# Hybrid state-space and attention block: three portions of a group's small work, at the ends of whole weight pieces

## The chip, the cores and the metric

The kernel runs on one core of one Trainium2 chip. The time is that of one execution in device microseconds (us), given as the median of several runs; the profile is of one execution. PE is the engine that multiplies matrices (PEld its weight loads), DVE is VectorE, ACT is ScalarE, POOL is GpSimd, and SP issues the DMAs.

## The reference

One transformer-like block over 512 tokens of width 1024, in float32. The part that the change touches is the state space branch; around it stand a three-group dilated attention, two gates and a feed-forward part with a short convolution.

```python
h = rms_norm(x, norm1_g)
z, xbc, dt_raw, q, k, v, g_ssd, g_attn = jnp.split(h @ w_in, IN_SPLITS, axis=-1)
# state space branch, 8 groups of 4 heads of 64, state 128, chunks of 128 tokens
xbc = silu(causal_dwconv(xbc, conv_w, conv_b))          # xs, Bm, Cm
dt = softplus(dt_raw + dt_bias)
CB = einsum('bclgn,bcsgn->bcgls', Cc, Bc)               # per group and chunk
y_diag = einsum('bcgkls,bcsgkp->bclgkp', CB[:, :, :, None] * Ldec, X)
states = einsum('bclgn,bcgkl,bclgkp->bcgkpn', Bc, decay_states, X)
prev = scan over the chunks: carry * chunk_decay + states
y_off = einsum('bclgn,bcgkpn,bcgkl->bclgkp', Cc, prev, exp(a_cs))
y = (y_diag + y_off + d_skip * xs) * silu(z)
y_ssd = rms_norm over each group's 256 channels
# the rest
merged = sigmoid(g_ssd) * (y_ssd @ w_ssd_proj) + sigmoid(g_attn) * (y_attn @ w_attn_proj)
x = x + merged @ w_out
x = x + (silu(u_gate) * u_val) @ w_down                 # u: convolved rms_norm(x) @ w_up
```

## The kernel before

**Large matmuls.** All weights come in pieces (512 KB here). SP loads a piece (`raw`, three buffers), ACT rounds it to `whi` (L104), and DVE takes the rest, `wlo = raw - whi` (L105); both have three buffers and are made up to two pieces ahead (`prefetch`). The activations are split into `hh` and `hl` in the same way. A piece of 128 output channels is then 24 matmuls of 128x128 by 512 tokens into one of four PSUM banks "mm": whi with hh, whi with hl, wlo with hh, eight each (`mm_chan`, L144).

**The state space stage.** The loop over `g` (8 groups) takes six pieces a group: B, C, two of x, two of z (`ps_ssd`). At the end of a piece, ACT and DVE bring the result out of PSUM; for B, C and x this is the convolution (`conv4`: one step on ACT, three on DVE, the latter shown as L52). Silu follows per pair (`silus`). Behind the eight groups stand 16 gate pieces (`ps_gate`); the first six of them are still run beside the small work, and then `finish` runs what is left of it.

**The small work of a group** is the generator `ssd_side`, with ps_cb (C with B, L714), ps_bt and ps_xt (transposes of B and x, L720 and L733), ps_st (states, L745), ps_y and ps_o (the two parts of the result for each half j, L764 and L769: y0, o0, y1, o1) and ps_n (the sum of squares for the norm, L785 and L786). The DVE steps between them are the subtraction that begins the decay matrix (`bc`, also called `mt` and `m4`, L705), `cbm` (L715), the product of the two (L723), `xdt` and `xdc` (L736, L739), the recurrence `prev` (L750 to L754) and four steps per half of y (L52, L772 to L774). ACT does Relu and Exp on the decay (L707, L708). The PSUM banks of the small work are two "tr" and two "aux".

**What sets the order.** PE runs its instructions in exactly the order in which the program is written (`manual_schedule` names PE). For the other engines and SP's queue, a scheduler at build time lays down an order from its own estimate of when operands are there, with the program's order as priority. All engines then work through their own list in order.

**Ticks.** Small work is put between large matmuls by `tick`, which advances every active generator whose wait is over; `yield k` means "go on k ticks later". A piece has two ticks, one after its 12th matmul and one at its end. Counted from a group's first piece, odd ticks fall into the middle of a piece, even ones at its end; 1 to 12 lie in the group's own pieces and 13 to 24 in those of the next group. With `GN = (7, 2, 2)`, `YL` and `NL`, a group from the third on has: 1 subtraction, 2 Relu and Exp, 9 cb and bt, 10 product, 12 and 13 xt, 14 st, 16 y0 and o0, 19 y1 and o1, 21 the decay loads for the group two further on (`load_decay`, one of 1 MB and two of 256 KB, two buffers each) and the sum of squares on POOL, 22 its split `sr`, 25 n, 27 and 28 the DMA back and the power on POOL. The first two groups start late and have numbers of their own (`G0`, `G1`), and the third starts four ticks late (`G2W`). The combination of the three attention groups (`combine`) starts `COMB` ticks after the last attention chain; it consists of 12 products with loaded factors (L645), 8 sums (L647) and 4 splits (L651 and L653), with the transposes ps_fT ahead of them. It runs beside the first groups of the state space stage.

Of the kernel before, what the change touches and what calls it, by code (L numbers as in the profile page):

```python
# [16 lines left out]
P = 128  # L17
S = 512
NT = S // P
# [4 lines left out]

LAG, PVLAG = 2, 2
LAUNCH = (12, 5, 13)
COMB = 11
G0, G1, GN = (2, 1, 1, 1), (5, 2, 4, 2), (7, 2, 2)
G2W, YL = 4, 3
NL = (1, 3, 2, 1)  # L30

Z0, XS0, B0, C0, DT0 = 0, 2048, 4096, 5120, 6144
Q0, K0, V0, GS0, GA0 = 6176, 7712, 9248, 10784, 11808
# [5 lines left out]
def kernel(  # L39
# [6 lines left out]
    nc = tc.nc  # L46
# [649 lines left out]
    def ssd_side(g, bct, xst, zs, at):  # L696
        sp = late["b"]

        def T(tag, shape, bufs=1):
            return sp.tile(shape, F32, tag=tag, name=f"{tag}_{g}", bufs=bufs)  # L700

        hs = slice(4 * g, 4 * g + 4)
        mt, eb = decay[g]
        m4 = mt.rearrange("p h (c l) -> p h c l", c=NT)
        nc.vector.tensor_sub(m4, acs[:, :, hs].rearrange("p c h -> p h c").unsqueeze(3).broadcast_to((P, 4, NT, P)), m4)  # L705
        yield 1
        nc.scalar.activation(mt, mt, AF.Relu)  # L707
        nc.scalar.activation(mt, mt, AF.Exp, scale=-1.0)  # L708
        yield at["cb"]
        cbm = T("cbm", [P, NT, P])  # L710
        ps = bank("aux", f"ps_cb{g}")
        for c in range(NT):
            cs = slice(c * P, (c + 1) * P)
            nc.tensor.matmul(ps[:, cs], bct[:, 0, cs], bct[:, 1, cs], start=True, stop=True)  # L714
        nc.vector.tensor_mul(cbm, ps.rearrange("p (c l) -> p c l", c=NT),  # L715
                             triu.unsqueeze(1).broadcast_to((P, NT, P)))
        btok = T("btok", [P, 3, P])
        ps = bank("tr", f"ps_bt{g}")
        for c in range(3):
            nc.tensor.transpose(ps[:, c * P:(c + 1) * P], bct[:, 0, c * P:(c + 1) * P], ident)  # L720
        nc.scalar.copy(btok.rearrange("p c n -> p (c n)"), ps[:, :3 * P])
        yield 1
        nc.vector.tensor_mul(m4, m4, cbm.unsqueeze(1).broadcast_to((P, 4, NT, P)))  # L723
        yield at["x"]
        xdt = T("xdt", [P, NT, 4, 64])
        xdc = T("xdc", [P, 3, 4, 64])
        for hf in range(2):
            ps = bank("tr", f"ps_xt{g}_{hf}")
            for c in range(2):
                for j in range(2):  # L730
                    o = c * 256 + j * P
                    t0 = (2 * hf + c) * P
                    nc.tensor.transpose(ps[:, o:o + P], xst[:, j, t0:t0 + P], ident)  # L733
            p4 = ps.rearrange("p (c h d) -> p c h d", c=2, h=4)
            cc = slice(2 * hf, 2 * hf + 2)
            nc.vector.tensor_mul(xdt[:, cc], p4, dtt[:, cc, hs].unsqueeze(3).broadcast_to((P, 2, 4, 64)))  # L736
            n = 2 - hf
            cc = slice(2 * hf, 2 * hf + n)
            nc.vector.tensor_mul(xdc[:, cc], p4[:, :n], dtd[:, cc, hs].unsqueeze(3).broadcast_to((P, n, 4, 64)))  # L739
            yield 1  # L740
        prev = T("prev", [P, 3, 4, 64])
        pst = [bank("aux", f"ps_st{g}_{i}") for i in range(2)]
        sts = [pst[c // 2][:, c % 2 * 256:c % 2 * 256 + 256] for c in range(3)]
        for c in range(3):
            nc.tensor.matmul(sts[c], btok[:, c, :], xdc[:, c].rearrange("p h d -> p (h d)"),  # L745
                             start=True, stop=True)
        for c in range(3):
            p3 = sts[c].rearrange("p (h d) -> p h d", h=4)
            if c == 0:
                nc.vector.tensor_copy(prev[:, 0], p3)  # L750
            else:
                nc.vector.tensor_mul(prev[:, c], prev[:, c - 1],
                                     cdec[:, c, hs].unsqueeze(2).broadcast_to((P, 4, 64)))
                nc.vector.tensor_add(prev[:, c], prev[:, c], p3)  # L754
        yield at["y"]
        sq = T("sq", [P, 2, S])
        for j in range(2):
            b = 2 * g + j
            y = ysb[:, b, :]
            psy = bank("aux", f"ps_y{g}_{j}")  # L760
            for c in range(NT):
                cs = slice(c * P, (c + 1) * P)
                for i in range(2):
                    nc.tensor.matmul(psy[i * 64:(i + 1) * 64, cs], xdt[:, c, 2 * j + i, :],  # L764
                                     mt[:, 2 * j + i, cs], start=True, stop=True)
            pso = bank("aux", f"ps_o{g}_{j}")
            for c in range(1, NT):
                cs = slice(c * P, (c + 1) * P)
                nc.tensor.matmul(pso[:, cs], prev[:, c - 1, 2 * j:2 * j + 2, :].rearrange("p h d -> p (h d)"),  # L769
                                 bct[:, 1, cs], start=True, stop=True)  # L770
            stt(y, xst[:, j, :], dsk[:, b:b + 1], psy, ALU.mult, ALU.add)
            nc.vector.tensor_mul(sq[:, j, P:], pso[:, P:], eb[:, j, P:])  # L772
            nc.vector.tensor_add(y[:, P:], y[:, P:], sq[:, j, P:])
            nc.vector.tensor_mul(y, y, zs[:, j, :])  # L774
            nc.scalar.activation(sq[:, j, :], y, AF.Square)
            yield YL - j
        load_decay(g + 2)
        nc.gpsimd.tensor_add(sq[:, 0, :], sq[:, 0, :], sq[:, 1, :])
        yield NL[0]
        sr = sp.tile([P, 2, S], F32R, tag="sr", name=f"sr_{g}", bufs=1)  # L780
        nc.scalar.copy(sr[:, 0, :], sq[:, 0, :])
        nc.gpsimd.tensor_sub(sr[:, 1, :], sq[:, 0, :], sr[:, 0, :].bitcast(F32))
        yield NL[1]
        ps = bank("aux", f"ps_n{g}")
        nc.tensor.matmul(ps[0:1, :], ones_r, sr[:, 0, :], start=True, stop=False)  # L785
        nc.tensor.matmul(ps[0:1, :], ones_r, sr[:, 1, :], start=False, stop=True)  # L786
        vv = T("vv", [1, S])
        nc.scalar.activation(vv, ps[0:1, :], AF.Identity, bias=epsb[0:1], scale=1.0 / 256)
        nc.sync.dma_start(scr_v[g], vv)
        yield NL[2]  # L790
        rv = T("rv", [P, NT], 2)
        nc.sync.dma_start(rv, scr_v[g].rearrange("(p c) -> p c", c=NT))
        yield NL[3]
        nc.gpsimd.tensor_tensor(rv, rv, nhalf.broadcast_to((P, NT)), op=ALU.pow)
        nc.sync.dma_start(scr_r[g].rearrange("(p c) -> p c", c=NT), rv)
# [3 lines left out]
            nc.scalar.activation(o, o, AF.Silu)  # L799
        yield 1  # L800

    normal = dict(zip(("cb", "x", "y"), GN))
    tiles = {}

    def branch_tiles(g):
# [3 lines left out]
    for g in range(8):  # L809
        if g > 1:  # L810
            branch_tiles(g)
        if g > 1:
            start(ssd_side(g, *tiles[g], normal), G2W if g == 2 else 0)
        banks = []
        for i in range(6):
            w = next_piece()
            banks.append(bank("mm", f"ps_ssd{g}_{i}"))
            mm_chan(banks[i], w, hh, hl)
            if (g, i) == (0, 1):
                ab_cm.__exit__(None, None, None)  # L820
                late["a"] = sa_cm.__enter__()
                branch_tiles(0)
            if (g, i) != (0, 0):
                bct, xst, zs = tiles[g]
                for k in ((0, 1) if (g, i) == (0, 1) else (i,)):
                    if k < 2:
                        conv4(banks[k], 16 + 8 * k + g, bct[:, k, :])
                    elif k < 4:
                        conv4(banks[k], 2 * g + k - 2, xst[:, k - 2, :])
                    else:  # L830
                        nc.scalar.copy(zs[:, k - 4, :], banks[k])
            if i % 2 and g > 0:
                start(silus(tiles[g][i // 2]), 1)
            tick()
            if (g, i) == (0, 4):
                assert not any(s[0].__name__ in ("chain", "launch") for s in sides)
                aa_cm.__exit__(None, None, None)
                ap = ap_cm.__enter__()
                for k in "hl":
                    merged[k] = ap.tile([P, 4, S], F32R, tag="a" + k, name="a" + k)  # L840
                sb_cm = pool("ssd_b", side="right")
                late["b"] = sb_cm.__enter__()
                load_decay(0)
                load_decay(1)
                start(ssd_side(0, *tiles[0], dict(zip(("cb", "x", "y"), G0))), G0[3])
            if (g, i) == (0, 5):
                start(ssd_side(1, *branch_tiles(1), dict(zip(("cb", "x", "y"), G1))), G1[3])
                start(silus(*tiles[0]), 1)


# [572 lines left out]
```

## Time and profile before

| | |
|---|---|
| median of 3 runs | 1215.61 us (1214.03 to 1215.69) |
| profiled execution | 1215.73 us, span 1214.0 us |
| busy PE / PEld | 1201.3 / 1001.8 us |
| busy DVE / ACT / POOL | 756.7 / 574.4 / 140.9 us |
| mean granted clock of PE | 0.996 |
| HBM traffic | 133.22 MB read, 4.70 MB written, 114 GB/s |

A view of groups or of the timeline names line, engine, operation, what is written and read (out<-in, by the program's names), the shapes and the count. "idle before" is time in which the engine had nothing under way, and what follows the arrow is what ended it. A matmul in full float32 appears as two records, one for each pass; the large ones are of a rounded type and appear as one. The end of a matmul is modelled and reaches past the start of the next, so that a row of n matmuls is measured better from start to start. The chain of waits follows the work that ended last back through the execution, and its pieces are laid end to end.

### The profile page before, as it was taken

Reading aid. Unit: us, or ns where it says so; the run is one execution under the profiler, and the core shown is the slowest. Engines: PE = TensorE matmul, PEld = TensorE weight load, DVE = VectorE, ACT = ScalarE, POOL = GpSimd, SP = SyncE. Lnnn points to the kernel's source line nnn. Section 1 sums busy time; section 2 is a strip of 40 time slices with the busy share of each in tenths; the row PEclk is TensorE's granted clock in tenths of the full one; section 3 lists DMA queues with packets and bytes.
Section 4 is the critical chain, followed back from the end, with each engine's and each line's share of the span. In section 5 each row is a group of like instructions: output and inputs, shape, how many; then the busy total and the mean of one; then the engine's idle time right before and its main releaser. Section 6 shows DMA issues by size and latency. Waiting matters only on the chain.

```text
span 1214.0 us, 15957 instructions
## 1 busy us (share of the span) xinstructions
PE 1201.3 (99%) x6316; PEld 1001.8 (83%) x6316; DVE 756.7 (62%) x999; ACT 574.4 (47%) x890; POOL 140.9 (12%) x95
## 2 busy tenths in 40 slices
PE   9999989999999999999999999999999999999998
PEld 7877767998888888888888888888888999988887
DVE  5214354356789977777744354654779888885542
ACT  4434456367746655465433333433554444444431
POOL 1011111100000201101011000000224242300000
PEclk9999989999999999999999999999999999999999
DMA  5444534422646544424235423344324242425330
GB/s 185 122 106 97 129 97 108 106 72 71 178 126 179 149 121 122 139 71 139 74 81 133 130 88 103 98 143 159 124 76 129 82 114 85 122 87 174 104 121 35
DMA packets 177163, 138.95 MB, mean 114 GB/s; under 512 B 12416, under 2 KB 150256, under 8 KB 176065
## 3 DMA queue, kind: packets, MB, share of 16 engines
q1 hardware_dynamic: 177089, 137.94, 40.2%
q8 instruction: 49, 0.80, 0.3%
q14 instruction: 25, 0.20, 0.1%
HBM read 133.22 MB, written 4.70 MB: 114 GB/s over the span
## 4 chain that ended last, share of the span: by engine, by line
PE 94%; DVE 2%; DMA 1%; ACT 1%; POOL 1%; issue 1%; SPq 0%; DVEq 0%; ACTq 0%; POOLq 0%
PE ps_ssd L144 22%; PE ps_wd L952 10%; PE ps_qk L144 10%; PE ps_u L1281 8%; PE ps_gate L144 7%; PE ps_sp L919 7%; PE ps_v L408 6%; PE ps_wo L952 3%; PE ps_uc L1108 2%; PE ps_ub L1108 2%; PE ps_ua L1108 2%; PE ps_u L144 2%; PE ps_ap L144 2%; PE ps_y L764 1%; PE ps_pv L579 1%; PE ps_s L537 1%
## 5 line engine op out<-in xcount | busy, mean ns | idle before, releaser
L105 DVE TENSOR_TENSOR wlo<-raw,whi 128x1024 fp32r<-128x1024 f32 x154 | 194.6, 1265 | 282.6 <-ACT whi L104 186.9
L104 ACT CAST whi<-raw 128x1024 fp32r<-128x1024 f32 x154 | 161.6, 1050 | 301.9 <-PE ps_ssd L144 62.1
L144 PE MATMUL ps_ssd<-hl,whi 128*128 128x512 f32 x384 | 102.9, 397 | 0.0
L144 PE MATMUL ps_ssd<-hh,whi 128*128 128x512 f32 x384 | 98.4, 398 | 0.0
L144 PE MATMUL ps_ssd<-hh,wlo 128*128 128x512 f32 x384 | 95.4, 390 | 0.0
L952 PE MATMUL ps_wd<-whi,asp 128*128 128x512 f32 x336 | 89.8, 389 | 0.0
L144 PEld LDWEIGHTS ps_ssd<-hh,wlo 128*128 128x128 f32 x384 | 72.1, 188 | 15.9
L144 PEld LDWEIGHTS ps_ssd<-hh,whi 128*128 128x128 f32 x384 | 70.6, 188 | 14.0 <-issue 0.2
L144 PEld LDWEIGHTS ps_ssd<-hl,whi 128*128 128x128 f32 x384 | 70.2, 188 | 14.1 <-issue 0.3
L952 PEld LDWEIGHTS ps_wd<-whi,asp 128*128 128x128 f32 x336 | 63.1, 188 | 13.1
L556 ACT ACTIVATE s<-s,st 128x128 f32<-128x128 f32 (+1 forms) x96 | 39.9, 417 | 37.5 <-DVE st L550 19.7
L952 PE MATMUL ps_wd<-wlo,asp 128*128 128x512 f32 x168 | 51.7, 389 | 0.0
L144 PE MATMUL ps_qk<-hh,whi 128*128 128x512 f32 x192 | 51.1, 409 | 0.0
L1156 ACT ACTIVATE facc<-facc 128x512 f32<-128x512 f32 x22 | 13.9, 633 | 76.1 <-DVE facc L52 76.1
L507 POOL TENSOR_TENSOR hrv<-hrv,nhalf 128x32 f32<-128x32 f32 x6 | 32.5, 5423 | 146.9 <-DMA hrv<-scr_q 146.9
L144 PE MATMUL ps_qk<-hl,whi 128*128 128x512 f32 x192 | 47.7, 390 | 0.0
L144 PE MATMUL ps_qk<-hh,wlo 128*128 128x512 f32 x192 | 47.4, 389 | 0.0
L1092 DVE TENSOR_TENSOR ulo<-rawup,uhi 128x1024 fp32r<-128x1024 f32 x31 | 44.5, 1435 | 4.5 <-ACT uhi L1086 4.5
L144 PEld LDWEIGHTS ps_qk<-hh,whi 128*128 128x128 f32 x192 | 35.9, 194 | 12.7 <-issue 4.5
L1281 PE MATMUL ps_u<-h2h,uhi 128*128 128x512 f32 x176 | 43.7, 390 | 0.0
L1281 PE MATMUL ps_u<-h2l,uhi 128*128 128x512 f32 x176 | 43.5, 389 | 0.0
L1281 PE MATMUL ps_u<-h2h,ulo 128*128 128x512 f32 x176 | 43.5, 389 | 0.0
(317 smaller groups left out, 2491.0 us busy)
## 6 DMA issues: line engine op xcount, KB each, us to landing
raw<-in_w_in_dram SPq DMA_DIRECT2D x100, 512.0 KB
rawup<-in_w_up_dram SPq DMA_DIRECT2D x40, 512.0 KB
raw<-in_w_down_dram SPq DMA_DIRECT2D x22, 512.0 KB
bc<-scr_a SPq DMA_DIRECT2D x8, 1024.0 KB
raw<-in_w_ssd_proj_dram SPq DMA_DIRECT2D x16, 512.0 KB
hrb<-scr_q SPq DMA_DIRECT2D x12, 512.0 KB
eb<-scr_e SPq DMA_DIRECT2D x16, 256.0 KB
raw<-in_w_out_dram SPq DMA_DIRECT2D x8, 512.0 KB
```

Source lines behind the costliest of these rows:

```text
L104: nc.scalar.copy(hi, raw)
L105: nc.vector.tensor_sub(lo, raw, hi.bitcast(F32))
L144: nc.tensor.matmul(ps[:, t0:t0 + nt], a[:, k, c:c + n], b[:, k, t0:t0 + nt], start=(i == 0), stop=(i == total - 1))
L408: nc.tensor.matmul(pss[b], tok(g, kq * 2 + k, b, xx), w[:, k, :], start=(kq == 0 and j == 0 and k == 0), stop=(kq == 3 and j == 2 and k == 1))
L507: nc.gpsimd.tensor_tensor(rv, rv, nhalf.broadcast_to((P, 32)), op=ALU.pow)
L556: nc.scalar.activation(s[:, o:o + nk * P], s[:, o:o + nk * P], AF.Exp, bias=st[:, q, 0, 2 * j + h:2 * j + h + 1], accum_out=st[:, q, 1, 2 ...
L919: nc.tensor.matmul(pss[j], w[:, k, cs], ys[k][xi], start=(k2 == 0 and i == 0 and k == 0), stop=(k2 == 7 and i == 2 and k == 1))
L952: nc.tensor.matmul(pss[b], xs(k0 + k, i)[:, b * P:(b + 1) * P], ww[:, k, :], start=(k0 == 0 and j == 0 and k == 0), stop=(k0 == nk - 2 and ...
L1092: nc.vector.tensor_sub(lo, source(m, x), hi.bitcast(F32))
L1108: nc.tensor.matmul(ba[m][bk][:, c * H:(c + 1) * H], a[:, k, :], b[:, k, :], start=(i == 0), stop=(i == 11))
L1156: nc.scalar.activation(facc[m], facc[m], AF.Silu)
L1281: nc.tensor.matmul(pss[i], a[:, k, :], b[:, k, :], start=(n == 0), stop=(n == 23))
```

## The change

Nothing is computed differently. `ssd_side` now has three portions of PE work and the norm: portion a (bt, both xt, cb, in this order) at tick 14, the end of the next group's first piece; st at 16; y0, o0, y1 and o1 together at 20. The product of decay and cbm is at 15, the next decay loads and the sum of squares at 23, `sr` at 25, n at 28, the DMA back and the power at 30 and 31. xdc is written ahead of xdt. The second xt goes to an "aux" bank, the second half of y and n to "tr" banks. The first two groups have their own numbers for the same three portions, the third starts with the others, and the combination of attention starts three ticks later.

```diff
-COMB = 11
-G0, G1, GN = (2, 1, 1, 1), (5, 2, 4, 2), (7, 2, 2)
-G2W, YL = 4, 3
-NL = (1, 3, 2, 1)
+COMB = 14
+G0, G1, GN = (3, 4, 1), (10, 4, 2), (12, 4)
+NL = (2, 3, 2, 1)
...
         nc.scalar.activation(mt, mt, AF.Exp, scale=-1.0)
-        yield at["cb"]
+        yield at["a"]
+        btok = T("btok", [P, 3, P])
+        ps = bank("tr", f"ps_bt{g}")
+        for c in range(3):
+            nc.tensor.transpose(ps[:, c * P:(c + 1) * P], bct[:, 0, c * P:(c + 1) * P], ident)
+        nc.scalar.copy(btok.rearrange("p c n -> p (c n)"), ps[:, :3 * P])
+        xdt = T("xdt", [P, NT, 4, 64])
+        xdc = T("xdc", [P, 3, 4, 64])
+        for hf in range(2):
+            ps = bank(("tr", "aux")[hf], f"ps_xt{g}_{hf}")
+            for c in range(2):
+                for j in range(2):
+                    o = c * 256 + j * P
+                    t0 = (2 * hf + c) * P
+                    nc.tensor.transpose(ps[:, o:o + P], xst[:, j, t0:t0 + P], ident)
+            p4 = ps.rearrange("p (c h d) -> p c h d", c=2, h=4)
+            n = 2 - hf
+            cc = slice(2 * hf, 2 * hf + n)
+            nc.vector.tensor_mul(xdc[:, cc], p4[:, :n], dtd[:, cc, hs].unsqueeze(3).broadcast_to((P, n, 4, 64)))
+            cc = slice(2 * hf, 2 * hf + 2)
+            nc.vector.tensor_mul(xdt[:, cc], p4, dtt[:, cc, hs].unsqueeze(3).broadcast_to((P, 2, 4, 64)))
         cbm = T("cbm", [P, NT, P])
         ps = bank("aux", f"ps_cb{g}")
...
         nc.vector.tensor_mul(cbm, ps.rearrange("p (c l) -> p c l", c=NT),
                              triu.unsqueeze(1).broadcast_to((P, NT, P)))
-        btok = T("btok", [P, 3, P])
...
         yield 1
         nc.vector.tensor_mul(m4, m4, cbm.unsqueeze(1).broadcast_to((P, 4, NT, P)))
-        yield at["x"]
-        xdt = T("xdt", [P, NT, 4, 64])
...
-            yield 1
+        yield 1
         prev = T("prev", [P, 3, 4, 64])
...
-            psy = bank("aux", f"ps_y{g}_{j}")
+            psy = bank(("aux", "tr")[j], f"ps_y{g}_{j}")
...
-            pso = bank("aux", f"ps_o{g}_{j}")
+            pso = bank(("aux", "tr")[j], f"ps_o{g}_{j}")
...
             nc.scalar.activation(sq[:, j, :], y, AF.Square)
-            yield YL - j
+        yield 3
         load_decay(g + 2)
...
-        ps = bank("aux", f"ps_n{g}")
+        ps = bank("tr", f"ps_n{g}")
...
-    normal = dict(zip(("cb", "x", "y"), GN))
+    normal = dict(zip(("a", "y"), GN))
...
-            start(ssd_side(g, *tiles[g], normal), G2W if g == 2 else 0)
+            start(ssd_side(g, *tiles[g], normal))
...
-                start(ssd_side(0, *tiles[0], dict(zip(("cb", "x", "y"), G0))), G0[3])
+                start(ssd_side(0, *tiles[0], dict(zip(("a", "y"), G0))), G0[2])
...
-                start(ssd_side(1, *branch_tiles(1), dict(zip(("cb", "x", "y"), G1))), G1[3])
+                start(ssd_side(1, *branch_tiles(1), dict(zip(("a", "y"), G1))), G1[2])
```

More of the change, by code (lines that the diff above doesn't have):

```diff
@@ L716, in ssd_side @@
                              triu.unsqueeze(1).broadcast_to((P, NT, P)))
-        btok = T("btok", [P, 3, P])
[L718 to L721, printed above, removed]
         yield 1
         nc.vector.tensor_mul(m4, m4, cbm.unsqueeze(1).broadcast_to((P, 4, NT, P)))
-        yield at["x"]
-        xdt = T("xdt", [P, NT, 4, 64])
[L726 to L739, printed above, removed]
-            yield 1
+        yield 1
         prev = T("prev", [P, 3, 4, 64])
```

## The prediction

> **What bounds the kernel.** I read the page first, then the busy time by stretches (us; each engine's busy time with its instruction count in brackets, then granted clock, share of the DMA engines, GB/s), then the waits.
>
> ```profile
> PE 1201.3 (99%) x6316; PEld 1001.8 (83%) x6316; DVE 756.7 (62%) x999; ACT 574.4 (47%) x890; POOL 140.9 (12%) x95
> ```
>
> ```profile
> core 0: us, PE busy (x) PEld busy (x) DVE busy (x) ACT busy (x) POOL busy (x), PEclk, DMA share, GB/s
> 363.00:407.00 44.00, 44.00 (x232) 35.98 (x231) 42.40 (x62) 25.57 (x30) 6.50 (x4) 1.00 0.70 193
> 482.30:522.80 40.50, 40.50 (x218) 33.22 (x217) 30.68 (x38) 23.46 (x26) 3.81 (x3) 1.00 0.42 119
> 806.00:904.00 98.00, 95.03 (x482) 80.54 (x481) 61.21 (x77) 43.44 (x66) 15.18 (x10) 1.00 0.41 135
> ```
>
> ```profile
> ACT whi L104 <- PE ps_ssd L144: 62.1, 21, 4.9
> ```
>
> PE is busy for the whole of both stretches of the state space stage, at the full clock; what idle it has lies elsewhere, 3 us of it between 806 and 904. VectorE has 10 us to spare in a steady group (482.30 to 522.80), but only 1.6 us of 44 where the attention groups are combined (363 to 407). The last row says that the split of the next weights waited 62 us in all for PE to free the old ones: the weights are ahead of PE, not behind it. So the time of this stage is the length of PE's instruction stream, and a change of order can gain only what PE loses around the small work, and lose only by making PE wait.
>
> A busy PE row hides what an interruption costs, so next comes the chain of waits over one steady group (start, us, what), with the gate stage as the undisturbed pace:
>
> ```profile
> 472.70 0.89 PE ps_cb L714 x8
> 473.59 0.33 PE ps_bt L720 x3
> 473.92 8.20 PE ps_ssd L144 x36
> 482.12 0.44 PE ps_xt L733 x4
> 482.56 2.76 PE ps_ssd L144 x12
> 485.32 0.23 PE ps_n L785
> 485.56 0.23 PE ps_n L786
> 485.78 0.44 PE ps_xt L733 x4
> 486.22 2.77 PE ps_ssd L144 x12
> 488.99 1.29 PE ps_st L745 x6
> 490.28 5.46 PE ps_ssd L144 x24
> 495.75 1.02 PE ps_y L764 x16
> 496.77 0.86 PE ps_o L769 x6
> 497.64 8.20 PE ps_ssd L144 x36
> 505.84 1.02 PE ps_y L764 x16
> 506.87 0.86 PE ps_o L769 x6
> 507.73 5.48 PE ps_ssd L144 x24
> 513.21 0.89 PE ps_cb L714 x8
> ...
> 643.38 54.43 PE ps_gate L144 x240
> ```
>
> A group takes 513.21 - 472.70 = 40.51 us. The pace is 54.43/240 = 0.2268 us a matmul, so the 144 large matmuls need 32.66 us. The other 7.85 us are the small rows themselves (0.89+0.33+0.44+0.23+0.23+0.44+1.29+1.02+0.86+1.02+0.86 = 7.61) and what the large matmuls lose just after each interruption: 8.20 - 36 x 0.2268 = 0.035 after cb and bt, 0.04 after the first xt, 0.05 after the second, 0.02 after st, 0.035 and 0.04 after the two y. I call these tails; together 0.22.
>
> **The change part by part.** No instruction is added or removed on any engine, DMAs included; durations and tile sizes stay. With ticks counted from a group's own first piece (odd: after half a piece; even: at its end; 13 and on lie in the next group), it moves: cb and bt from 9 to 14, the two xt from 12 and 13 to 14, the product of decay and cbm from 10 to 15, st from 14 to 16, y0 from 16 and y1 from 19 both to 20, the next decay loads and the sum of squares from 21 to 23, sr from 22 to 25, the norm's matmuls from 25 to 28, and the DMA of rv and the power behind it from 27 and 28 to 30 and 31.
>
> PE, portion a (bt, xt, xt, cb). Three interruptions (cb and bt; xt; xt beside n) become one; n moves over to st, where a tail is paid anyway. Gain: two tails of about 0.045, 0.09 a group.
>
> PE, y0 and y1 in one. One tail of 0.035 goes. What y costs on entry is not in the tails: 8 pairs of passes at 0.109 (0.44/4) are 0.87, and the row says 1.02. Does that entry go too when y1 follows o0 instead of a large matmul? No row shows o followed by y. The nearest are a large matmul followed by y, and, elsewhere, a short full-array matmul followed by one on a part of the columns (timeline: start, duration):
>
> ```profile
> 115.46 0.27 PE L364 MATMUL ps_acsT<-ident,ysb 128*128 128x128 f32 x1
> 115.66 1.06 PE L499 MATMUL ps_hs<-qsq,heads 128*32 128x512 f32 x8
> ...
> 493.77 1.98 PE L144 MATMUL ps_ssd<-hh,wlo 128*128 128x512 f32 x8
> 495.68 1.09 PE L764 MATMUL ps_y<-bc,xdt 128*64 128x128 f32 x16
> ```
>
> From 493.77 to 495.68 is 1.91, eight matmuls are 1.81: 0.10 lost before y. From acsT to hs is 0.20, where a full-array pass takes 0.11 (0.44/4 for xt): 0.09 lost there too. The loss belongs to the change of column shape, not to leaving the large stream, so I take it as unchanged (gain 0). The ends: all of the entry gone, 1.02 - 0.87 = 0.15 a group; or, at worst, a second entry's 0.15 on top. The Trainium skill, "TensorEngine Tiling (Array Packing)", section "Key Properties", says that changing the tiling mode drains the engine. By that rule y0, o0, y1, o1 have the same four changes as before and the merge brings only its tail; the rival reading, that the drain is paid for leaving the large stream, would make the sum 1.2 us lower. The two pairs of rows above side with the rule, as far as two pairs can.
>
> PE's sum: (0.09 + 0.035) x 8 groups = 1.0 us gained, between 2.2 (entry free, 8 x 0.15 more) and -0.2 (entry doubled).
>
> PSUM banks. Portion a now needs both "tr" and both "aux" banks at once, y all four. Their last users are two or more pieces back (y at 20, n and st at 16, a at 14), except that st takes the two banks which xt1 and cb left one piece earlier. Cost 0, but that cover is thin and decides the rival below. Had y1 kept "aux", it would have waited for y0's VectorE chain; with "tr" it waits for nothing.
>
> VectorE between portion a and st. The rows (timeline: start, duration; in brackets idle time before and what ended it):
>
> ```profile
> 473.55 3.36 DVE L705 TENSOR_TENSOR bc<-acs,bc 128x2048 f32<-128x2048 f32 x1 [1.59 <-DMA bc<-scr_a]
> 476.84 0.73 DVE L52 SCALAR_TENSOR_TENSOR xst<-ps_ssd,sc,xst 128x510 f32<-128x510 f32 x1
> 477.50 0.67 DVE L715 TENSOR_TENSOR cbm<-ps_cb,triu 128x512 f32<-128x512 f32 x1
> ...
> 486.57 0.68 DVE L736 TENSOR_TENSOR xdt<-ps_xt,dtt 128x512 f32<-128x512 f32 x1
> 487.17 0.42 DVE L739 TENSOR_TENSOR xdc<-ps_xt,dtd 128x256 f32<-128x256 f32 x1
> 489.78 1.22 DVE L105 TENSOR_TENSOR wlo<-raw,whi 128x1024 fp32r<-128x1024 f32 x1 [2.19 <-ACT whi L104]
> ```
>
> At the end of the first piece VectorE meets one wlo (1.22), the convolution's three steps (3 x 0.73 = 2.2) and portion a's four products and cbm (0.68 x 3 + 0.42 + 0.67, in all 3.1, and some 0.1 less for each that starts before the last ends): 6.0 to 6.5 us. It can start when bt and the first xt are through, 0.33 + 0.44 and the 0.16 by which a pass outlasts its turn (0.27 - 0.11 at acsT), so 0.9 us after portion a begins, and is done at about 7.3. PE needs the products at 2.1 (portion a) + 5.44 (24 matmuls) + 0.46 (n, ahead of st) = 8.0. Slack 0.7 us: no wait in a steady group. What is queued behind a late product on PE is everything, since PE keeps the written order.
>
> VectorE after y. Both y chains, about 5 us, now meet in one piece, with the fourth piece's convolution and a wlo: 5 + 2.2 + 1.2 = 8.4 us in 5.44 + 3.8 = 9.2 of PE. Large matmuls need none of it for two pieces and more (four "mm" banks, weights split two pieces ahead: wlo in the row above starts when the cast is done, not when PE asks). Cost 0; without that lead it would be some 3 us a group.
>
> The decay loads. SP issues bc when y1's matmuls have read the old tile (SP's queue, start and duration of the issue):
>
> ```profile
> 466.39 0.33 SPq L689 DMA_DIRECT2D bc<-scr_a  x1
> ```
>
> One period later that is 506.90, where the row of y1 ends (505.84 + 1.02). The subtraction at 473.55 waited for this load, so it landed 473.55 - 466.39 = 7.2 us after issue. It will now be issued half a piece (2.7) and y0's 1.9 later, 4.6 us. Its work is due at the product of tick 15, a group and more after that. Raw loads queued behind this wait on SP are covered by the lead that the whi row shows. VectorE, if it stands at the subtraction early, holds wlo back, with that same lead. Cost 0; if the lead is gone, up to those 4.6 us a group.
>
> The combination of the attention groups starts 3 ticks later (14 for 11). Its 12 products, 8 sums and 4 differences go by this row (groups of instructions, 365 to 412: busy, mean ns):
>
> ```profile
> L645 DVE TENSOR_TENSOR ysb<-ysb,fb 128x512 f32<-128x512 f32 x12 | 7.8, 686 | 0.0
> ```
>
> 24 x 0.69 = 16.5 us of VectorE, in the stretch that has 1.6 us spare. It ends 1.5 pieces later and so meets portion a of group 2, which no longer starts 4 ticks late. Its last block is six operations, 4.1 us, beside the 6.3 that have 0.7 of slack. If it goes first, st of group 2 waits 4.1 - 0.7 = 3.4 us, once; if last, 0. I take 0.6, near the lower end: this stretch of before was as full, and PE has no idle in its row.
>
> The last group's norm. Its n stands after the sixth gate piece, now two pieces behind the end of y1 (10.9 us) where it was two and a half (13.6). PE did not wait for it before, so the wait now lies between 0 and 2.7 us; I take 0, since the other end needs that it was only just in time before.
>
> Sum: -1.0 + 0.6 = -0.4 us. The profiled execution took 1215.73 (span 1214.0), so 1215.3; the median of the runs, 1215.61, is 0.12 below it: **1215.2**.
>
> **Rivals.**
> 1. Slower: st waits for VectorE in every group. Place: PE's st, one piece after portion a. It decides from 0.7 us of extra VectorE work in that piece. A candidate is the decay subtraction (3.36 in the row above), if it slips in ahead of the products: 3.4 - 0.7 = 2.7 in seven groups, 18.9 us, 1215.2 + 18.9 = 1234; in one or two groups, 1218 to 1221. Against: that load lands in the two pieces where VectorE is now emptier.
> 2. The entry to y is free after o: 8 x 0.15 = 1.2 less, 1214.0. Against it stand the acsT rows.
> 3. Faster by more: with rival 2, and with the later stages' order shifting so that part of the 3 us of idle PE between 806 and 904 goes: 1212.5. Nothing in the change reaches there.
> 4. The portions don't bind what they name: only PE keeps the written order. The subtraction at 473.55 already ran about 12 us ahead of its tick (1, the middle of a first piece, where n stands at 485.32). Then VectorE's order hardly changes, st meets no wait, and PE's gain stands alone: 1215.61 - 1.0 = 1214.6.
>
> **Numbers.** 0.2% is 2.43 us, about what a measurement of this kernel tells from no change: below 1213.2 is faster, above 1218.0 slower. Chances: the forecast with rival 4 (1214.0 to 1217), 0.61; rival 2, 0.12; rival 3, 0.07; rival 1 in all groups 0.08, in one or two 0.12. The first two are "same": 0.73; faster 0.07; slower 0.20. Range 1213.0 to 1219.5: it takes in the entry's ends and a wait in one group, leaving out most of rival 3, and rival 1 in several groups.
>
> **What would show it.** The chain over a steady group should have three interruptions instead of six, a period of 40.4 us, cb's row next to bt and xt, and the second y row still at 1.0 us. Wrong: an idle PE or PEld before st with VectorE's xdc, xdt or cbm as its releaser (rival 1), a second y row near 0.87 (rival 2), or PE idle before n of the last group or before a y.

## The result and the profile after

The changed kernel took 1223.41 us (median of 4 runs, 1220.99 to 1226.4), the kernel before 1215.31 (4 runs, 1214.03 to 1215.69): ratio 1.007, interval 1.0046 to 1.0093. It is slower, and outside the predicted range of 1213.0 to 1219.5. The profiled execution took 1223.19 (span 1221.5).

The page's busy times, to be set beside those of before:

```profile
PE 1200.5 (98%) x6316; PEld 1002.9 (82%) x6316; DVE 751.9 (62%) x999; ACT 573.9 (47%) x890; POOL 150.8 (12%) x95
```

PE is busy 0.8 us less in a span that is 7.5 us longer: PE waits somewhere. POOL has 10 us more with the same 95 instructions; that is the trail to the cause. Next the busy time by stretches, a disturbed one and the steady group that the prediction showed:

```profile
core 0: us, PE busy (x) PEld busy (x) DVE busy (x) ACT busy (x) POOL busy (x), PEclk, DMA share, GB/s
402.00:442.00 40.00, 35.24 (x186) 28.73 (x185) 34.98 (x50) 22.57 (x25) 7.18 (x3) 0.96 0.54 151
482.30:522.80 40.50, 40.50 (x217) 33.38 (x216) 30.91 (x38) 22.29 (x25) 4.88 (x3) 1.00 0.43 118
```

In the steady group PE is as full as before; near 415 it is idle for 4.8 us, and the clock is below 1. The chain of waits over a steady group (start, us, what):

```profile
473.98 1.02 PE ps_y L762 x16
475.00 0.86 PE ps_o L767 x6
475.87 1.02 PE ps_y L762 x16
476.89 0.86 PE ps_o L767 x6
477.75 16.34 PE ps_ssd L143 x72
494.10 0.33 PE ps_bt L712 x3
494.43 0.87 PE ps_xt L722 x8
495.30 0.89 PE ps_cb L733 x8
496.19 5.49 PE ps_ssd L143 x24
501.68 0.23 PE ps_n L783
501.92 0.23 PE ps_n L784
502.15 1.39 PE ps_st L743 x6
503.53 10.90 PE ps_ssd L143 x48
514.44 0.58 PE ps_y L762 x7
```

Three interruptions instead of six, as the change says. The tails behind them are 16.34 - 72 x 0.2268 = 0.01, 5.49 - 5.44 = 0.05 and 0.01: together 0.07, where before had 0.22. The period here is 514.44 - 473.98 = 40.46; st's row is 0.10 longer than the 1.29 of before, and without that it would be 40.36. (In the last two groups st's row is 1.29 again; from st of the one to st of the other, 582.93 to 623.30, it is 40.37.)

Now the disturbed group, the timeline of PE (start, duration; in brackets idle before and what ended it):

```profile
414.26 0.40 PE L783 MATMUL ps_n<-sr,ones_r 128*1 128x512 f32 x1
419.64 2.90 PE L743 MATMUL ps_st<-xdc,btok 128*128 128x256 f32 x6 [4.76 <-DVE xdt L728]
421.98 2.56 PE L143 MATMUL ps_ssd<-hh,whi 128*128 128x512 f32 x8
```

From n at 414.26 to the first large matmul behind st, 421.98, 7.7 us pass, against 503.53 - 501.68 = 1.85 in the steady group; with the slower matmuls behind st it costs 6.5. It is the only wait of 0.3 us and more that the waits of PE show in this stage.

From the first ps_ssd to the first ps_sp the stage takes 452.67 us, against 447.31 before: +5.36, which is 6.5 for this one place less 1.1 gained over the groups. The other 2.06 us of the profiled difference lie ahead of the stage: the first ps_ssd starts at 274.15 instead of 272.09. All engines run the same order up to there, and in the profiles of the kernels below, which share that part too, the start lies anywhere from 270.73 to 273.48: run variation of the attention stage, not the change. So "stage" in the table below is the cleaner measure.

**Why st came late.** The waits between 400 and 430:

```profile
ACT sr L779 <- POOL sq L776: 7.5, 1, 7.5
PE ps_st L743 <- DVE xdt L728: 4.8, 1, 4.8
DVE al L652 <- ACT ah L650: 3.0, 2, 2.4
```

PE waits for VectorE, VectorE has waited for ACT, and ACT for POOL, which adds the two halves of group 1's squares (timeline of POOL):

```profile
397.33 7.29 POOL L776 TENSOR_TENSOR sq<-sq 128x512 f32<-128x512 f32 x1 [3.20 <-ACT sq L773]
446.25 1.29 POOL L776 TENSOR_TENSOR sq<-sq 128x512 f32<-128x512 f32 x1 [20.73 <-ACT sq L773]
```

The same addition takes 1.30 and 1.29 us for groups 0 and 2, and 7.29 for group 1. In the kernel before, group 1's took longer too, but only 3.37:

```profile
401.07 3.37 POOL L778 TENSOR_TENSOR sq<-sq 128x512 f32<-128x512 f32 x1 [16.10 <-ACT sq L775]
```

The timeline of VectorE meanwhile, in the changed kernel:

```profile
397.05 1.88 DVE L644 TENSOR_TENSOR ysb<-ysb,fb 128x512 f32<-128x512 f32 x3
...
401.20 2.28 DVE L704 TENSOR_TENSOR bc<-acs,bc 128x2048 f32<-128x2048 f32 x1
405.83 1.37 DVE L652 TENSOR_TENSOR al<-ysb,ah 128x512 fp32r<-128x512 f32 x1 [2.36 <-ACT ah L650]
...
413.56 0.42 DVE L726 TENSOR_TENSOR xdc<-ps_xt,dtd 128x256 f32<-128x256 f32 x1
413.90 1.23 DVE L104 TENSOR_TENSOR wlo<-raw,whi 128x1024 fp32r<-128x1024 f32 x1
415.04 0.74 DVE L51 SCALAR_TENSOR_TENSOR bct<-ps_ssd,sc,bct 128x511 f32<-128x511 f32 x1
415.70 0.68 DVE L644 TENSOR_TENSOR ysb<-ysb,fb 128x512 f32<-128x512 f32 x1
...
418.22 0.68 DVE L644 TENSOR_TENSOR ysb<-ysb,fb 128x512 f32<-128x512 f32 x1
418.82 0.68 DVE L728 TENSOR_TENSOR xdt<-ps_xt,dtt 128x512 f32<-128x512 f32 x1
```

VectorE runs without a pause, steps with two inputs in SBUF all of them, until 403.47; POOL's addition ends at 397.33 + 7.29 = 404.62, which is 1.15 later, nearly the whole of its usual 1.29. So POOL, it seems, got nowhere until VectorE paused. ACT, which stood at `sr`, could not make the combination's `ah` (VectorE idle 2.36). Then the combination's last products and sums, pushed back, stand between the convolution's steps (L51) and ahead of the last `xdt`, which ends at 419.50; st starts at 419.64.

Why st waits for `xdt` deserves a second look, for it does not read it. By its row it reads `xdc`, whose last part was done at 413.97, and `btok` (timeline of ACT):

```profile
414.44 0.47 ACT L713 COPY btok<-ps_bt 128x384 f32<-128x384 f32 x1
```

Both were there at 414.91. What ties st to `xdt`, by the kernel's text, is a PSUM bank: st writes into the two "aux" banks, one of which held the second xt, and `xdt` is the last to read that. In the kernel before, both xt stood in "tr" banks. No run here gives st another bank, so how much of the wait would go with it is not shown.

There are two possible causes for the late `xdt`: too much VectorE work in front of it, and the lockout of POOL. The experiments had to part them.

### The profile page after: what moved, and what is told of

The parts are those of the page before. It is cut to its first block, busy times and chain, and to the rows that moved or that the text cites. A ratio compares the mean times of both kernels' runs of the same rounds, so it can differ in the third digit from the quotient of the medians.

```text
span 1221.5 us, 15951 instructions
## 1 busy us (share of the span) xinstructions
PE 1200.5 (98%) x6316; PEld 1002.9 (82%) x6316; DVE 751.9 (62%) x999; ACT 573.9 (47%) x890; POOL 150.8 (12%) x95
## 4 chain that ended last, share of the span: by engine, by line
PE 90%; DVE 3%; DMA 2%; POOL 2%; ACT 2%; issue 1%; SPq 0%; DVEq 0%; POOLq 0%; ACTq 0%
PE ps_ssd L143 20%; PE ps_wd L950 10%; PE ps_u L1279 8%; PE ps_qk L143 8%; PE ps_gate L143 7%; PE ps_sp L917 7%; PE ps_v L407 5%; PE ps_wo L950 3%; PE ps_uc L1106 2%; PE ps_ub L1106 2%; PE ps_ua L1106 2%; PE ps_u L143 2%; PE ps_ap L143 2%; PE ps_y L762 1%; DMA hrb<-scr_q 1%; PE ps_pv L578 1%
## 5 line engine op out<-in xcount | busy, mean ns | idle before, releaser
L143 PE MATMUL ps_ssd<-hl,whi 128*128 128x512 f32 x384 | 96.1, 391 | 0.0
L776 POOL TENSOR_TENSOR sq<-sq 128x512 f32<-128x512 f32 x8 | 17.5, 2185 | 228.2 <-ACT sq L773 228.2
```

What stands on the lines that cost most here:

```text
L143: nc.tensor.matmul(ps[:, t0:t0 + nt], a[:, k, c:c + n], b[:, k, t0:t0 + nt], start=(i == 0), stop=(i == total - 1))
```

## Experiments

All times beside runs of the kernel before on the same chip; "idle" is PE's wait in the stage, "stage" the time from first ps_ssd to first ps_sp (447.31 before, 452.67 after).

| run | median us | ratio (interval) | idle PE, us | stage us |
|---|---|---|---|---|
| e8, after unchanged | 1220.86 | 1.0042 (1.0027 to 1.0057) | st of group 2: 5.74 | 453.80 |
| e1, combination at 10 | 1221.52 | 1.0047 (1.0032 to 1.0063) | st 2: 3.65; st 6: 1.88 | 454.69 |
| e2, sum of squares on VectorE | 1218.66 | 1.0042 (1.0011 to 1.0072) | st 2: 2.89 | 452.52 |
| e4, before with combination at 14 | 1221.95 | 1.0049 (1.0031 to 1.0068) | st 2: 2.43 + 0.74 | 453.64 |
| e5, e1 and e2 together | 1215.06 | 0.9994 (0.9983 to 1.0006) | st 2: 0.90 | 447.30 |
| e3, group 2 late | 1219.24 | 1.0034 (1.0023 to 1.0045) | xt 2: 6.98; st 2: 1.68; st 6: 0.55 | 457.73 |
| e6, st a piece later | 1222.55 | 1.0055 (1.0042 to 1.0067) | y 2: 3.97; o 2: 0.48 | 454.26 |
| e7, e5 and e6 together | 1220.88 | 1.0043 (1.003 to 1.0055) | y 1: 4.48; o 1: 0.55 | 454.11 |
| e9, e5 and st 2 half a piece later | 1214.33 | 0.999 (0.9979 to 1.0) | none over 0.3 | 446.35 |
| e10, combination at 6 | 1213.59 | 0.9985 (0.9972 to 0.9999) | st 1: 0.38 | 446.89 |

**e1: the combination four ticks earlier.**

```diff
-COMB = 14
+COMB = 10
```

> The changed kernel with the combination of attention started 4 ticks earlier (10 instead of 14), nothing else. Theory A: the third group's states wait because the sum of squares of group 1 on POOL could not run beside VectorE's unbroken row of two-input steps (7.29 us where it takes 1.29), and ACT, whose next step needs that sum, stood for 7.5 us, so that everything behind it on ACT and then on VectorE came late. Theory B: VectorE is simply full there; the combination's steps stand in its list ahead of the products of portion a, and POOL is a bystander. Both expect the wait before st of group 2 (4.8 us idle, 6.5 us in all with the slow restart) to go: 1223.4 - 6.5 = 1216.9, with 1215 to 1218. Should it stay above 1221, the place of the combination is not the cause. The first 272 us hold the same instructions in the same order as in the kernel before; if the 2 us by which the changed kernel was late there come from run to run, some of these runs will have them and some not.

Most of the loss stayed. The waits of e1 from 380 to 440:

```profile
PE ps_st L743 <- DVE xdt L728: 3.7, 1, 3.7
ACT sr L779 <- POOL sq L776: 6.1, 1, 6.1
```

and VectorE's timeline:

```profile
410.39 0.69 DVE L652 TENSOR_TENSOR al<-ysb,ah 128x512 fp32r<-128x512 f32 x1 [3.96 <-ACT ah L650]
```

Here VectorE's amount of work is not the limit: it stood still for 3.96 us, for ACT, which stood for POOL (sum of squares 5.88 us). The products of portion a stand behind `al` in VectorE's list. The lockout, with one step of the combination left behind it, keeps PE waiting 3.65 us. The 1.88 at group 6 is another matter: there the decay load landed 8.5 us after its issue, where it took 5.2 in after, and VectorE's subtraction, ACT's Relu and Exp, the casts behind them and so wlo and `xdt` came late.

**e2: group 1's sum of squares on VectorE, the combination left at 14.**

```diff
-        nc.gpsimd.tensor_add(sq[:, 0, :], sq[:, 0, :], sq[:, 1, :])
+        (nc.vector if g == 1 else nc.gpsimd).tensor_add(sq[:, 0, :], sq[:, 0, :], sq[:, 1, :])
```

> The changed kernel with the sum of squares of group 1 alone on VectorE instead of POOL. This separates the two theories: A expects ACT's wait of 7.5 us for that sum to shrink to 1 us or less and the wait before st of group 2 to fall from 4.8 us to below 2: 1217 to 1219.5. B expects the wait to stay or to grow by the 0.7 us that VectorE does more: 1222.5 to 1225.

ACT no longer waits for POOL, and yet (waits, and the busy time of the stretch ahead of st):

```profile
PE ps_st L743 <- DVE xdt L728: 2.9, 1, 2.9
410.00:415.00 5.00, 2.11 (x11) 1.23 (x9) 5.00 (x9) 3.70 (x5) 0.00 (x0) 0.93 0.78 202
415.00:420.00 5.00, 5.00 (x12) 4.01 (x13) 5.00 (x6) 0.04 (x1) 3.58 (x1) 0.50 0.39 105
```

VectorE (the fourth figure) is busy throughout while PE (the first after the length) is idle for 2.89 of the first five. So VectorE's full list alone keeps PE waiting too: `xdc` was done at 408.13, but the last `xdt`, behind steps of the combination and the convolution, only at 414.85, and st starts at 414.99. (The sum itself puts 0.69 us more on VectorE here.) The times varied a good deal (1214.5 to 1231.0); the profile carries the point.

**e4: the kernel before, with nothing but the combination at 14.**

```diff
-COMB = 11
+COMB = 14
```

> The kernel before with the combination 3 ticks later (14 instead of 11) and nothing else. Both theories: without the portions and with group 2 still 4 ticks late, the combination meets no product that PE waits for: 1214.5 to 1216.5, no idle PE between 272 and 806. If it loses 3 us or more, the later combination costs by itself.

That one number costs the kernel before as much as the whole change costs: 1.0049 against 1.007 and, in e8, 1.0042. Its busy time by stretches around st of group 2:

```profile
405.00:410.00 5.00, 5.00 (x23) 4.11 (x22) 5.00 (x7) 1.78 (x3) 0.00 (x0) 1.00 0.50 154
420.00:425.00 5.00, 2.14 (x5) 1.17 (x4) 5.00 (x8) 2.70 (x4) 0.82 (x1) 0.74 0.39 105
425.00:430.00 5.00, 4.69 (x13) 3.76 (x14) 4.90 (x10) 0.53 (x1) 0.00 (x0) 0.58 0.37 105
```

VectorE is full from 405 on, and POOL's sum takes 1.5 us with nobody waiting for it. So neither the three portions nor the lockout are needed for a loss of this size: moving the combination of attention three ticks later is enough. Here st waits for `xdc`, which it reads.

**e5: both causes taken away** (the edits of e1 and e2 together).

> The changed kernel with the combination 4 ticks earlier and the sum of squares of group 1 on VectorE, both at once. The first four runs left two theories that each explain one of them: with the sum on VectorE, ACT's wait went and PE still waited 2.9 us, because VectorE was busy without a break (full); with the combination earlier, VectorE stood idle 4.0 us for ACT, which waited for POOL. If both conditions are needed for st of group 2 to be in time, this kernel has no wait there: the stage from the first state space matmul to the first of the ssd projection takes 446 to 447 us instead of 452.7, and the time is 1214 to 1216.5. If VectorE is too full even then, 1 to 3 us of idle PE remain, with 1.7 or 3.4 us of half clock behind them: 1218 to 1221.

The wait shrinks to 0.90 us, the clock keeps 1.00, and the stage is as long as before: both together explain the loss. The gain of PE's stream is not yet seen, since these 0.9 eat most of it.

**e9: e5, and st of group 2 alone half a piece later.**

```diff
-        yield 1
+        yield 2 if g == 2 else 1
         prev = T("prev", [P, 3, 4, 64])
...
-        yield at["y"]
+        yield at["y"] - (g == 2)
```

> The kernel that was level with the one before (combination at 10, group 1's sum of squares on VectorE) with st of group 2 alone half a piece later (tick 17, in the middle of a piece; its y stays at 20). It still had 0.9 us of idle PE before that st; half a piece is 2.7 us of slack more. The theory of a used-up slack expects that idle to go and nothing to take its place: the stage 446.2 us instead of 447.3, 1213.5 to 1215, so 0.1% below the kernel before, hardly more than these runs can tell. The rival that the delay only moves on expects idle before y of group 2, 1216 to 1219.

No wait is left, and the stage is 446.35, 0.96 shorter than before. This is the gain that the prediction had as 1.0.

**e10: only the combination, at 6,** the sum left on POOL.

```diff
-COMB = 14
+COMB = 6
```

> The changed kernel with the combination 8 ticks earlier (6 instead of 14) and the sum of squares left on POOL. The theory that both the lock-out of POOL and the full VectorE come from the combination running beside y of group 1 and portion a of group 2 expects both to go together: group 1's sum on POOL below 3 us (7.3 in the changed kernel), ACT's wait for it below 2 us, no idle PE before st of group 2; stage 446 to 447, time 1214 to 1216. If the combination only moves the crowd to y of group 0 and portion a of group 1, idle PE shows there instead, before st or y of group 1, and the time is 1217 to 1222.

The fastest of all, by 0.15% (0.01% to 0.28%) under the kernel before. Its busy time in the stretch of the trouble:

```profile
395.00:430.00 35.00, 35.00 (x193) 29.00 (x192) 29.75 (x40) 20.38 (x23) 4.92 (x3) 1.00 0.57 142
```

and the same 35 us of after:

```profile
395.00:430.00 35.00, 30.24 (x137) 24.70 (x136) 31.89 (x44) 18.72 (x23) 11.84 (x3) 0.95 0.52 137
```

VectorE has 5.25 us to spare, POOL is busy 4.92 instead of 11.84 (the sum takes 2.62), and PE has no gap. The stage is 0.42 shorter than before. The rest of the 1.9 us by which the median is lower is not shown to be the change: the profile's first ps_ssd is at 271.12, 0.97 earlier than in the profile of before, within the variation of the attention stage. Another 1.4 lies behind the stage: there the profile of before has PE at half clock from 903.0 to 906.5 (0.51), and e10's has not (1.00). The profiles of e1 to e4, e6 and e7 have no such stretch either, those of after, e5, e8 and e9 have one, so it does not go with the combination's place.

**e6 and e7: more room ahead of st in all groups.** st stands a piece later (e6), and the same with e5's edits (e7).

```diff
-G0, G1, GN = (3, 4, 1), (10, 4, 2), (12, 4)
+G0, G1, GN = (3, 2, 1), (10, 2, 2), (12, 2)
...
-        yield 1
+        yield 3
         prev = T("prev", [P, 3, 4, 64])
```

> The changed kernel with st one piece later in every group (tick 18 instead of 16, y still at 20), combination and POOL as they are. The prediction gave the products 0.7 us of slack between portion a and st; this makes it 0.7 + 5.4 = 6.1. The theory that the loss is this slack, used up by whatever delays VectorE (its own load or ACT behind POOL), expects no idle PE at st of any group, also not the short ones of groups 4 and 5: stage 446 to 447 us, time 1213.5 to 1216. A rival: the delay only moves on to y, whose recurrence now has one piece less: idle PE before y of group 2, 1217 to 1221.

> Both of the last two together: st one piece later, the combination 4 ticks earlier, the sum of squares of group 1 on VectorE. As st one piece later alone if that has no wait left: 1213.5 to 1216, the stage 446 us. It is the version to beat the kernel before, by the 1.0 to 1.2 us that PE's stream is shorter; more than 2 us would need a gain that no step so far names.

Neither helped. The wait moved from st to y, behind the recurrence that st feeds. The waits of e6:

```profile
PE ps_y L762 <- DVE prev L752: 4.0, 1, 4.0
```

In e7 it is group 1's y, at 388.42. VectorE's timeline of e7 shows why:

```profile
385.46 0.41 DVE L748 COPY prev<-ps_st 128x256 f32<-128x256 f32 x1
385.79 0.68 DVE L646 TENSOR_TENSOR ysb<-ysb 128x512 f32<-128x512 f32 x1
386.39 0.41 DVE L750 TENSOR_TENSOR prev<-prev,cdec 128x256 f32<-128x256 f32 x1
386.73 1.22 DVE L104 TENSOR_TENSOR wlo<-raw,whi 128x1024 fp32r<-128x1024 f32 x1
387.86 0.41 DVE L752 TENSOR_TENSOR prev<-prev,ps_st 128x256 f32<-128x256 f32 x1
```

The recurrence's steps of 0.41 us come one at a time between sums of the combination and a wlo: a short chain on a full engine takes as long as what the scheduler puts between its links. The recurrence is due a piece after st in these two, and two pieces after it in after, which leaves it less room.

**e3: group 2 two ticks later.**

```diff
-            start(ssd_side(g, *tiles[g], normal))
+            start(ssd_side(g, *tiles[g], normal), 2 if g == 2 else 0)
```

> The changed kernel with group 2 started 2 ticks late (the kernel before had 4), so that its portion a comes one piece later, at the end of the second piece, with its states one piece after. B: the products meet less of the combination, the wait falls to below 2 us: 1217 to 1219. A: ACT stands at the same place as before, but has caught up by the time portion a comes: also below 2 us. If it stays above 3 us, the backlog is longer than one piece, and the removal of the late start is not what costs.

This one tells nothing of the question, for it made a new wait: n of group 1, bt and xt of group 2 now fall on one tick and share the two "tr" banks, and xt waited 6.98 us for ACT to read n. ACT had stood 8.5 us at `sr` for POOL's sum, and the sum behind a power that was locked out in its turn (timeline of POOL in e3; the same step took 1.36 in after):

```profile
390.45 10.49 POOL L792 TENSOR_TENSOR rv<-rv,nhalf 128x4 f32<-128x4 f32 x1 [32.19 <-DMA rv<-scr_v]
```

**e8: after once more.**

> The changed kernel once more, unchanged. The 2 us by which its profile was late before the state space stage have, in the five profiles so far, gone with the run (270.7 to 274.2 us with the same order of instructions). If so, this profile may begin the stage anywhere between 270 and 275, while the wait before st of group 2 comes back: 3 to 5 us idle, stage 451 to 455 us. Time 1221 to 1225.

The wait of st (5.74), POOL's sum (7.29 us, to the hundredth) and ACT's wait (7.5) came again, so they belong to the program and not to one run. Against runs of before on its own chip the kernel is 6.0 us slower by the medians (5.1 by the ratio), which the stage (453.80 - 447.31 = 6.5) accounts for.

## Why the prediction was wrong

The step that failed is the price of the combination: 0.6 us put down, 6.5 measured. Point by point, by its own steps:

- *PE, portion a* and *the tails*: right. The tails of a group are 0.07 instead of 0.22, a gain of 0.15 where 0.125 was put down; over the stage about 1.1 in after (6.5 - 5.36) and 0.96 in e9, for 1.0.
- *The entry to y*: right. The second y row is 1.02, as the first, so rival 2 falls and the pairs of rows were read rightly. The Trainium skill, "TensorEngine Tiling (Array Packing)", section "Key Properties", says that a change of the tiling mode drains the engine; 1.02 twice agrees with it.
- *VectorE after y, the decay loads, the last group's norm*: 0 each, and no wait of PE of 0.3 us or more is seen at any of them in after. A late decay load did cost 1.88 us in e1.
- *PSUM banks*: put at 0, with the remark that the cover at st's banks is thin. It is there that the wait ended in after and e2: st's operands were there, and it waited for `xdt` to free the second xt's bank. In e3 another bank bit as well, the "tr" bank that n held.
- *VectorE between portion a and st*, slack 0.7: too much, though it costs little. In the steady group above `xdt` ends just before st starts, and st's row is 0.10 longer: the slack is used up. e1's 1.88 us at group 6 says how thin the cover is.
- *The combination*: the step that failed. "If it goes first, st of group 2 waits 4.1 - 0.7 = 3.4 us, once; if last, 0. I take 0.6". It cost 6.5. Three things were wrong with it. The choice: "this stretch of before was as full, and PE has no idle in its row" was taken as a reason for the low end, but a row at 42.4 of 44 says that the next 4 us of work have no room; e4 shows the loss in the kernel before itself (st waits 2.43 and 0.74). The bound: 3.4 counted VectorE's own operations and left out that an unbroken VectorE keeps POOL out, and with it ACT, and so VectorE itself 2.36 us (e1 shows that path nearly by itself: 3.65). The price: idle was counted as idle, where PE also runs slower after it (below).
- *Rival 1* named the right place and the right releaser (st, waiting for VectorE, "in one or two groups, 1218 to 1221"), but with the decay subtraction as the cause, at 2.7 us a group. Its 0.12 was too little. Rival 4, that VectorE's order hardly changes, is wrong for the combination.

Between the two causes the split can't be given as one figure: taking one away left 3.65 (e1, though its combination was also moved) and 2.89 us (e2) of the 4.76 to 5.74, both together 0.90 (e5). They overlap; either is enough to keep PE waiting.

## What to carry to other kernels

When a change moves a block of work on an engine that is nearly full in that stretch, price it by the full end of the bound, and ask first what it pushes behind it: a row of 42.4 of 44 us is a warning, not a cover. Before believing in a rearrangement of one engine's stream, vary by itself each number that went with it: here the stream's gain of about 1 us was real, and a block of work beside it, in the wrong place, cost 6.5 us. No one value explains that: `COMB` at 14 loses as much in the kernel before (e4), at 10 the changed kernel still lost 0.47% (e1), at 6 it is level with the one before or 0.15% below it (e10); 11, the value of before, was not run with the three portions. Count among what a matmul waits for the last reader of the bank that it writes. And when a small step becomes more than five times as long with no more instructions, look at who shares its path to memory.

## What the hardware showed

**POOL locked out.** Two tensors of 128x512 are added in 1.29 us; beside VectorE steps without a pause, with two inputs in SBUF, it took 7.29 (twice, in after and e8), 5.88 (e1) and 2.62 (e10), and the power of 128x4 in e3 10.49 instead of 1.36. In after it ended 1.15 us after VectorE's row of such steps did (403.47), in e1 1.14 (406.43 and 407.57), in e10 1.15 (402.85 and 404.00). The Trainium skill, "SBUF — State Buffer", section "SBUF: two separate sides", says that VectorE, in a step with two inputs in SBUF, and GpSimd share a pair of ports as an exclusive lock, held for a whole instruction by whichever starts first. The rows agree with a lock; they suggest besides that it can pass from one VectorE instruction to the next, several times over, with POOL left waiting.

**The clock after a wait.** The granted clock falls when PE has stood still, and stays low while PE is busy again: 0.50 over a full five microseconds in e2. In stretches of half a microsecond it shows 1.00 or 0.50, and a value between only where it changes, so (1 - clock) x 2 x length gives the time at half speed: for e4, 0.26 x 2 x 5 + 0.42 x 2 x 5 = 6.8 us. In 0.9 of that PE was idle; half of the rest, 3.0, is lost on top of 2.43 + 0.74 idle, together 6.1, where its stage is 6.3 longer. For after, these stretches:

```profile
414.00:420.00 6.00, 1.24 (x5) 0.55 (x4) 6.00 (x9) 3.78 (x6) 0.00 (x0) 0.95 0.92 241
420.00:424.00 4.00, 4.00 (x13) 3.15 (x13) 4.00 (x5) 0.87 (x2) 1.73 (x1) 0.65 0.23 47
```

0.05 x 2 x 6 + 0.35 x 2 x 4 = 3.4 us at half speed, 0.3 of it idle, so 1.6 lost, on top of 4.76. Waits of 0.90 (e5) and 1.88 (e1, group 6) brought no fall. So where the clock falls, a wait near 3 us in this stream costs about twice its length. The Trainium skill, "TensorE: Matmul & The Clock Gate", section "What's actually happening", has the clock halved after at least one idle window of about 3.4 us, counted freely and not from a kernel's events. The 3.4 and 6.8 fit one and two such windows. A window that is idle from end to end does not fit e2: there the clock fell near 414.25, when PE had stood for 2.2 us, and the measurement decides.
